# Pools of their own for the hi and the lo tiles of the weights, with lo moved 32 bytes off a multiple of 64

## The chip, the cores and the metric

The kernel runs on one core of a Trainium2 chip. The metric is device microseconds of one execution. Besides the timed runs there is one profiled execution, from which all rows below come: TensorE (PE, with its weight loads as PEld), VectorE (DVE), ScalarE (ACT), GpSimd (POOL), and the DMA queue issued by SyncE (SP).

## The reference

A decoder trunk of two layers on one sequence of 256 tokens, model width 2048, all in float32:

```
for i in range(DEPTH):                       # DEPTH = 2
    h = rmsnorm(x, norm_mix_pre[i])
    m = ssd_mixer(h, ...) if i == 0 else diff_attention(h, ...)
    x = x + rmsnorm(m, norm_mix_post[i])
    h = rmsnorm(x, norm_ffn_pre[i])
    x = x + rmsnorm(swiglu(h, w_gate, w_up, w_down), norm_ffn_post[i])
```

Layer 0 mixes with a Mamba-2 state space block (inner width 4096, 64 heads, chunks of 128), layer 1 with differential attention (16 heads). Each is followed by a SwiGLU network of width 5632. Nearly all arithmetic is in the products of 256 rows with large weight matrices: the input and output projections of the state space block, q/k/v and the output of attention, gate, up and down twice.

## The kernel before

**Products in three parts.** A float32 operand is split into hi, its value rounded to the matmul type float32r, and lo, the rest. A product is hi·hi + hi·lo + lo·hi, three matmuls into the same PSUM accumulator. Activations are split once (`xT_hi`, `xT_lo`, and `ah`/`al` pieces), weights as they come in.

**Weights.** `load` (line 101) brings a block of 128 x 4 x 512 floats (1 MB) into a tile `raw`, of which there are three. `prep` (line 106) makes one hi and one lo tile of 128 x 2 x 512 from half of it: ScalarE writes hi (L113, or L117 where a scale is folded in), VectorE writes lo = raw - hi (L114, L118). Both tiles come from one pool, with four buffers each. In the first part of the kernel there is one such pool, `hlA`; once the state space scan is over and its scratch is given back, a second one, `hlB`, is opened in that place, and tiles are taken from the two in turn.

**Two forms of product.** `mv` (line 143) has the activations as the stationary operand (128 x 128) and the weights as the moving one, 512 columns: L153 runs the three matmuls (x hi, w hi), (x hi, w lo), (x lo, w hi) for each of two 128-row slices. `ws` (line 168) has it the other way round: a 128 x 128 piece of the weights is stationary, and x hi or x lo is moving, 256 columns (L183), in the order (w hi, x hi), (w hi, x lo), (w lo, x hi).

**Order.** The program is written out in full. The order of the work is that of the Python code: `tick` runs small deferred pieces (scan, softmax, transposes, norms) between the steps of the big products. Each engine works through its own list in order and waits for the tiles it needs; buffers come free when their last reader is done.

**Where the tiles lie.** Within a partition, the pools are laid one behind the other. The program of before gives these byte addresses:

| tile | starts at | modulo 64 |
|---|---|---|
| `mhalf`, `table` (4 bytes each) | 18528, 18560 | 32, 0 |
| `xT_hi`, `xT_lo` (4 x 4096 each) | 18944, 35328 | 0 |
| `ones` (512) | 51712 | 0 |
| `dg` (512) | 55264 | 32 |
| `ah`, `al` pieces (8 x 2048 each) | 73216, 89600 | 0 |
| `raw` (3 x 8192) | 105984 | 0 |
| first set: hi, lo (4 x 4096 each) | 130560, 146944 | 0, 0 |
| scan: `mt`/`xg` (5 x 4096), then 8 x 2048 | 163328, 183808 | 0, 0 |
| scan: `dtr` (1024); `u` (2 of 1036) | 203232; 216064, 217120 | 32; 0, 32 |
| later in the scan's place: x rows (8 x 2048), post weights (2 x 2048) | 163328, 179712 | 0, 0 |
| second set: hi, lo (4 x 4096 each) | 183808, 200192 | 0, 0 |
| work tiles of 512 floats (6 x 2048) | 216576 | 0 |

Two gap tiles (`gap1`, line 43, 56 floats; `gap0`, line 88, 88 floats) are there for their size alone.

Of the kernel before, what the change touches and what calls it, by code (L numbers as in the profile page):

```python
# [10 lines left out]
F32 = mybir.dt.float32  # L11
F32R = mybir.dt.float32r
# [4 lines left out]
P = 128  # L17
# [3 lines left out]
KD = D // P  # L21
DI = 4096
NH = 64
# [10 lines left out]
def trunk_kernel(ctx, tc, x_rows, x_cols, vec_cols, vec64, post_rows, lam_rows,  # L34
                 w_zxbc, w_dt, w_so, w_qkv, w_ao,
                 w_g0, w_u0, w_d0, w_g1, w_u1, w_d1, out):
    nc = tc.nc
# [7 lines left out]
    mpool = ctx.enter_context(tc.tile_pool(name="mpool", bufs=8))  # L45
    actp = ctx.enter_context(tc.tile_pool(name="actp", bufs=8))
    rawp = ctx.enter_context(tc.tile_pool(name="rawp", bufs=3))
    hlA = ctx.enter_context(tc.tile_pool(name="hlA", bufs=4))
    accp = ctx.enter_context(tc.tile_pool(name="accp", bufs=4, space=PSUM))
    auxp = ctx.enter_context(tc.tile_pool(name="auxp", bufs=4, space=PSUM))  # L50
    dramp = ctx.enter_context(tc.tile_pool(name="dramp", bufs=1, space=bass.MemoryType.DRAM))
# [42 lines left out]
        sl = slice(t * P, (t + 1) * P)  # L94
        return xT_hi[kt // 4][:, kt % 4, sl], xT_lo[kt // 4][:, kt % 4, sl]

    pools = {"hl": [hlA]}
    seq = [0]
    pending = deque()

# [5 lines left out]
    def prep(raw, scale=None):  # L106
        i = seq[0]
        seq[0] += 1
        pl = pools["hl"][i % len(pools["hl"])]
        hi = pl.tile([P, 2, 512], F32R, tag="hi", name=f"hi{i}")  # L110
        lo = pl.tile([P, 2, 512], F32R, tag="lo", name=f"lo{i}")
        if scale is None:
            nc.scalar.copy(hi, raw)  # L113
            nc.vector.tensor_tensor(lo, raw, hi.bitcast(F32), op=ALU.subtract)  # L114
        else:
            for j in range(2):
                nc.scalar.activation(hi[:, j], raw[:, j], AF.Copy, scale=scale[j])  # L117
                nc.vector.scalar_tensor_tensor(lo[:, j], raw[:, j], scale[j], hi[:, j].bitcast(F32),  # L118
                                               op0=ALU.mult, op1=ALU.subtract)
        return hi, lo  # L120
# [22 lines left out]
    def mv(blocks, stat, evac, lag, scale=None, loaded=()):  # L143
        acc = {}
        last = 2 * len(blocks) - 1

        def run(i, t, hi, lo):
            if i == 0:
                acc[t] = accp.tile([P, 512], F32, tag="acc", name="acc")
            for j in range(2):  # L150
                xh, xl = stat(i, j, t)
                for q, (a, b) in enumerate(((xh, hi), (xh, lo), (xl, hi))):
                    nc.tensor.matmul(acc[t], a, b[:, j], start=(i == 0 and j == 0 and q == 0),  # L153
                                     stop=(i == last and j == 1 and q == 2))
            if i == last:
                evac(t, acc[t])

        for i in range(last + 1):
            if i % 2 == 0:
                raw = loaded[i // 2] if i // 2 < len(loaded) else load(blocks[i // 2])  # L160
            e = 2 * (i % 2)
            hi, lo = prep(raw[:, e:e + 2], scale(i) if scale else None)
            run(i, 0, hi, lo)
            pending.append(lambda i=i, hi=hi, lo=lo: run(i, 1, hi, lo))
            flush(lag)
            tick()

    def ws(blocks, evac):
        flush()
        acc = [accp.tile([P, 512], F32, tag="acc", name="acc") for _ in range(4)]  # L170
        last = 2 * len(blocks) - 1
        for i in range(last + 1):
            if i % 2 == 0:
                raw = load(blocks[i // 2])
            e = 2 * (i % 2)
            hi, lo = prep(raw[:, e:e + 2])
            for ct in range(4):
                cs = slice(ct * P, (ct + 1) * P)
                for j in range(2):
                    kt = i * 2 + j  # L180
                    xh, xl = xT_hi[kt // 4][:, kt % 4], xT_lo[kt // 4][:, kt % 4]
                    for q, (w, xx) in enumerate(((hi, xh), (hi, xl), (lo, xh))):
                        nc.tensor.matmul(acc[ct][:, :S], w[:, j, cs], xx,  # L183
                                         start=(i == 0 and j == 0 and q == 0),
                                         stop=(i == last and j == 1 and q == 2))
                if i == last:
                    evac(ct, acc[ct][:, :S])
            tick()
# [45 lines left out]

    seq[0] += 1
    draw = rawp.tile([P, KD, NH], F32, tag="raw", name="dtraw")
    dhi = hlA.tile([P, KD, NH], F32R, tag="hi", name="dthi")
    dlo = hlA.tile([P, KD, NH], F32R, tag="lo", name="dtlo")
    pdt = accp.tile([P, 512], F32, tag="acc", name="pdt")
    sqs = s2.tile([P, 2, S], F32, tag="t2", name="sqs")  # L240
    for k in range(2):
# [278 lines left out]
    def out_proj(w, first, last, acts, kgs, step, final, lag, t512, pw, scale=None, ns=range(4)):  # L520

        def sums(t, n):
            mt = m[(t, n)]
            row_sumsq(ss4[t][:, n:n + 1], mt, t512("junk"))
            dst = t512("mw") if n == 3 else mt
            (nc.vector if n == 3 else nc.gpsimd).tensor_tensor(dst, mt, pw(n), op=ALU.mult)  # L526
            return dst

        ss4 = {}
        for n in ns:  # L530
            def evac(t, ps, n=n):
                if first:
                    m[(t, n)] = mpool.tile([P, 512], F32, tag="m", name="m")
                    nc.scalar.copy(m[(t, n)], ps)
                else:
                    nc.vector.tensor_tensor(m[(t, n)], m[(t, n)], ps, op=ALU.add)
                if not last:
                    return
                if t not in ss4:
                    ss4[t] = small.tile([P, 4], F32, tag="ss4", name="ss_m", bufs=3)  # L540
                    for e in range(n):
                        sums(t, e)
                dst = sums(t, n)
                if n == 2:
                    p3 = small.tile([P, 1], F32, tag="ss1", name="p3", bufs=3)
                    nc.vector.tensor_reduce(p3, ss4[t][:, 0:3], axis=AX.X, op=ALU.add)
                    nc.vector.tensor_scalar(ss4[t][:, 0:1], p3, 1.0 / D, EPS, op0=ALU.mult, op1=ALU.add)
                if n == 3:
                    norm_chain(t, ss4[t], dst, step, final, t512)

            def stat(i, j, t):
                hi, lo = lookup(acts, (t, kgs[i] // 2))
                jj = (kgs[i] % 2) * 2 + j
                return hi[:, jj], lo[:, jj]

            mv([w[n, kg // 2] for kg in kgs[::2]], stat, evac, lag,
               (lambda i: [scale[:, 2 * kgs[i] + j:2 * kgs[i] + j + 1] for j in range(2)]) if scale is not None else None)
# [27 lines left out]


    postp = ctx.enter_context(tc.tile_pool(name="postp", bufs=1))
    hlB = ctx.enter_context(tc.tile_pool(name="hlB", bufs=4))
    t5 = ctx.enter_context(tc.tile_pool(name="t5", bufs=6))

    def t512(name, shape=(P, 512)):
# [2 lines left out]
    def load_post(ix):  # L594
        def get(n):
            if n not in w:
                w[n] = postp.tile([P, 512], F32, tag="post", name="wpost", bufs=2)
                nc.sync.dma_start(w[n], post_rows[ix, n * 512:(n + 1) * 512].partition_broadcast(P))
            return w[n]

        w = {}
        return get
# [3 lines left out]
            xres[(t, n)] = postp.tile([P, 512], F32, name=f"x_{t}_{n}")  # L606
            nc.sync.dma_start(xres[(t, n)], x_rows[t, :, n * 512:(n + 1) * 512])

    pools["hl"] = [hlA, hlB]
    out_proj(w_so, False, True, ssd_act, list(range(8, 16)), 0, False, LAG, t512, load_post(0), ssd_norm, ns=range(1, 4))  # L610

    def u_stat(i, j, t):
# [199 lines left out]
```

## Time and profile before

| | |
|---|---|
| median of 2 runs | 2618.14 us (2617.39 to 2618.90) |
| the profiled execution | 2617.48 us, its span 2615.7 us |
| granted TensorE clock | 0.997 |
| busy: PE, DVE, ACT, POOL | 99%, 60%, 47%, 6% |
| DMA | 483.35 MB, 185 GB/s on average |

In a row of a group, the name `acc<-lo,xTh` says that the instruction writes tile `acc` and reads `lo` and `xTh`; then come the shapes, the count, the total busy time in us, the mean time of one in ns, and the time for which the engine sat idle just ahead of them, with what ended it. A row of one tile or line gives minimum, median and maximum in ns, and the first and last start in us. A row of waits reads: who waited, for whom, us in total, how many times, the longest. [...]

### The profile page before, as it was taken

To read this page: it belongs to the slowest core of one execution; us is meant where nothing else is said; L and a number is where in the kernel's file an instruction comes from. 1 tells how busy PE (TensorE), PEld (TensorE's weight loads), DVE (VectorE), ACT (ScalarE), POOL (GpSimd) and SP (SyncE) were. 2 spreads that over 40 slices of the span, in tenths; PEclk is the share of its full clock that TensorE was granted. 3 is DMA by queue.
4 is the path that set the end of the run, shared out by engine and by line. 5 is a ranking of instruction groups with operands and counts; after the bars stand their busy time and mean duration, and the time that the engine had idled before them with its cause. 6 is when DMAs were issued, how large, how long until landed. Compare 5 with 4: busy or idle time off the path is not lost.

```text
span 2615.7 us, 34002 instructions
## 1 busy us (share of the span) xinstructions
PE 2589.5 (99%) x13670; PEld 2195.3 (84%) x13670; DVE 1557.1 (60%) x2100; ACT 1241.0 (47%) x1686; POOL 155.6 (6%) x164
## 2 busy tenths in 40 slices
PE   8999999999999999999999999999999999999998
PEld 7988889888888888888888889997788888888886
DVE  8888648887664544455445765556654444555455
ACT  4555555555554444443444644444644444443443
POOL 2031000120100000000001100000100000000002
PEclk9999999999999999999999999999999999999999
DMA  6545555446645555555555543543555555555553
GB/s 223 194 150 199 180 197 179 176 170 218 214 180 193 191 187 193 186 193 193 193 186 192 201 148 143 194 161 136 172 207 193 188 193 187 188 193 193 189 187 131
DMA packets 86653, 483.35 MB, mean 185 GB/s; under 512 B 8096, under 2 KB 24800, under 8 KB 30176
## 3 DMA queue, kind: packets, MB, share of 16 engines
q1 hardware_dynamic: 85840, 480.35, 51.9%
q8 instruction: 107, 1.75, 0.3%
q10 hardware_dynamic: 656, 0.85, 0.1%
q14 instruction: 50, 0.41, 0.0%
HBM read 479.00 MB, written 2.16 MB: 184 GB/s over the span
## 4 chain that ended last, share of the span: by engine, by line
PE 95%; DVE 2%; ACT 1%; issue 1%; POOL 0%; DMA 0%; DVEq 0%; ACTq 0%; POOLq 0%
PE acc L153 73%; PE acc L183 17%; PE pt_f L198 1%; PE sc L688 1%; DVE lo L114 1%; DVE v L349 1%; PE py L424 1%; ACT hi L113 0%; DMA dtraw<-in_w_dt_dram 0%; ACT junk L209 0%; PE pyt L434 0%; ACT xTh L505 0%; PE px L411 0%; PE pst L451 0%; PE po L723 0%
## 5 line engine op out<-in xcount | busy, mean ns | idle before, releaser
L114 DVE TENSOR_TENSOR lo<-raw,hi 128x1024 fp32r<-128x1024 f32 x816 | 1022.1, 1255 | 876.9 <-ACT hi L113 876.1
L113 ACT CAST hi<-raw 128x1024 fp32r<-128x1024 f32 x816 | 856.8, 1052 | 1042.5 <-PE acc L153 813.2
L153 PE MATMUL acc<-hi,xTh 128*128 128x512 f32 x1792 | 710.9, 397 | 1.4 <-ACT xTh L505 1.4
L153 PE MATMUL acc<-hi,xTl 128*128 128x512 f32 x1792 | 704.0, 393 | 0.0
L153 PE MATMUL acc<-lo,xTh 128*128 128x512 f32 x1792 | 701.4, 392 | 2.3 <-DVE lo L114 2.3
L153 PEld LDWEIGHTS acc<-hi,xTh 128*128 128x128 f32 x1792 | 337.1, 188 | 76.2 <-ACT xTh L505 5.3
L153 PEld LDWEIGHTS acc<-lo,xTh 128*128 128x128 f32 x1792 | 337.5, 188 | 73.0 <-DVE lo L114 3.1
L153 PEld LDWEIGHTS acc<-hi,xTl 128*128 128x128 f32 x1792 | 337.0, 188 | 71.5 <-issue 1.3
L183 PE MATMUL acc<-xTh,hi 128*128 128x256 f32 x1280 | 365.9, 286 | 3.4 <-DVE u L345 3.4
L183 PE MATMUL acc<-xTl,hi 128*128 128x256 f32 x1280 | 362.6, 283 | 0.0
L183 PE MATMUL acc<-xTh,lo 128*128 128x256 f32 x1280 | 362.3, 284 | 0.0
L153 PE MATMUL acc<-hi,al_f 128*128 128x512 f32 x704 | 275.4, 391 | 0.0
L153 PE MATMUL acc<-lo,ah_f 128*128 128x512 f32 x704 | 274.3, 390 | 0.0
L153 PE MATMUL acc<-hi,ah_f 128*128 128x512 f32 x704 | 274.2, 390 | 0.0
L183 PEld LDWEIGHTS acc<-xTh,hi 128*128 128x128 f32 x1280 | 245.9, 192 | 4.6 <-DVE u L345 3.8
L183 PEld LDWEIGHTS acc<-xTl,hi 128*128 128x128 f32 x1280 | 245.9, 192 | 0.7 <-issue 0.5
L183 PEld LDWEIGHTS acc<-xTh,lo 128*128 128x128 f32 x1280 | 245.4, 192 | 0.1
L153 PEld LDWEIGHTS acc<-lo,ah_f 128*128 128x128 f32 x704 | 132.2, 188 | 27.5
L153 PEld LDWEIGHTS acc<-hi,al_f 128*128 128x128 f32 x704 | 132.3, 188 | 27.1
L153 PEld LDWEIGHTS acc<-hi,ah_f 128*128 128x128 f32 x704 | 132.3, 188 | 26.9
L118 DVE SCALAR_TENSOR_TENSOR lo<-raw,cols,hi 128x512 fp32r<-128x512 f32 x128 | 92.9, 764 | 61.7 <-ACT hi L117 61.5
L526 POOL TENSOR_TENSOR m<-m,wpost 128x512 f32<-128x512 f32 x24 | 37.1, 1544 | 1510.9 <-ACT junk L209 1503.3
(192 smaller groups left out, 2048.0 us busy)
## 6 DMA issues: line engine op xcount, KB each, us to landing
raw<-in_w_g_dram SPq DMA_DIRECT2D x88, 1024.0 KB, 4.7
raw<-in_w_u_dram SPq DMA_DIRECT2D x88, 1024.0 KB, 4.7
raw<-in_w_d_dram SPq DMA_DIRECT2D x88, 1024.0 KB, 4.8
raw<-in_w_zxbc_dram SPq DMA_DIRECT2D x80, 1024.0 KB, 4.8
raw<-in_w_qkv_dram SPq DMA_DIRECT2D x48, 1024.0 KB, 4.8
raw<-in_w_so_dram SPq DMA_DIRECT2D x32, 1024.0 KB, 4.8
raw<-in_w_ao_dram SPq DMA_DIRECT2D x16, 1024.0 KB, 4.8
mt<-acum_d SPq DMA_DIRECT2D x16, 512.0 KB, 6.6
```

Of the source, the lines that this page charges most:

```text
L113: nc.scalar.copy(hi, raw)
L114: nc.vector.tensor_tensor(lo, raw, hi.bitcast(F32), op=ALU.subtract)
L118: nc.vector.scalar_tensor_tensor(lo[:, j], raw[:, j], scale[j], hi[:, j].bitcast(F32), op0=ALU.mult, op1=ALU.subtract)
L153: nc.tensor.matmul(acc[t], a, b[:, j], start=(i == 0 and j == 0 and q == 0), stop=(i == last and j == 1 and q == 2))
L183: nc.tensor.matmul(acc[ct][:, :S], w[:, j, cs], xx, start=(i == 0 and j == 0 and q == 0), stop=(i == last and j == 1 and q == 2))
L198: nc.tensor.transpose(pt[:, j], src[:, j * P:(j + 1) * P], ident)
L349: nc.vector.scalar_tensor_tensor(v, u[:, k:k + S], cwh[:, ch, k:k + 1], v, op0=ALU.mult, op1=ALU.add)
L424: nc.tensor.matmul(py[e * 64:(e + 1) * 64, a], xd[c][:, 2 * a + e], mts[c][:, 2 * a + e], start=True, stop=True)
L526: (nc.vector if n == 3 else nc.gpsimd).tensor_tensor(dst, mt, pw(n), op=ALU.mult)
L688: nc.tensor.matmul(sc[c][:, h], qT[cp, h, ts], kT[cp, h, :nk * P], start=True, stop=True)
```

## The change

Each set of weight tiles now has one pool for hi and one for lo. Between them, and ahead of the second set, stands a pool with one tile of four floats. The first lo set so starts at 146976, 32 past a multiple of 64. All that lies behind it moves by 32 bytes too: the scan's tiles, then the x rows and post weights. In the second set two more such tiles bring hi to 183872, on a multiple of 64, and lo to 200288, 32 past one; the work tiles then start at 216672, 32 past one. Numbers of buffers, the order of the instructions and the tiles ahead of the first lo set (x, activations, raw, hi) stay as they were. The names of hi and lo tiles get an a or a b for the set.

```diff
-    hlA = ctx.enter_context(tc.tile_pool(name="hlA", bufs=4))
+    hiA = ctx.enter_context(tc.tile_pool(name="hiA", bufs=4))
+    offA = ctx.enter_context(tc.tile_pool(name="offA", bufs=1))
+    gapA = offA.tile([P, 4], F32, name="gapA")
+    nc.gpsimd.memset(gapA, 0.0)
+    loA = ctx.enter_context(tc.tile_pool(name="loA", bufs=4))
...
-    pools = {"hl": [hlA]}
+    pools = {"hl": [(hiA, loA)]}
...
-        hi = pl.tile([P, 2, 512], F32R, tag="hi", name=f"hi{i}")
-        lo = pl.tile([P, 2, 512], F32R, tag="lo", name=f"lo{i}")
+        ab = "ab"[i % len(pools["hl"])]
+        hi = pl[0].tile([P, 2, 512], F32R, tag="hi", name=f"hi{ab}{i}")
+        lo = pl[1].tile([P, 2, 512], F32R, tag="lo", name=f"lo{ab}{i}")
...
-    dhi = hlA.tile([P, KD, NH], F32R, tag="hi", name="dthi")
-    dlo = hlA.tile([P, KD, NH], F32R, tag="lo", name="dtlo")
+    dhi = hiA.tile([P, KD, NH], F32R, tag="hi", name="dthi")
+    dlo = loA.tile([P, KD, NH], F32R, tag="lo", name="dtlo")
...
-    hlB = ctx.enter_context(tc.tile_pool(name="hlB", bufs=4))
+    offB = ctx.enter_context(tc.tile_pool(name="offB", bufs=1))
+    gapB = offB.tile([P, 4], F32, name="gapB")
+    nc.gpsimd.memset(gapB, 0.0)
+    hiB = ctx.enter_context(tc.tile_pool(name="hiB", bufs=4))
+    offC = ctx.enter_context(tc.tile_pool(name="offC", bufs=1))
+    gapC = offC.tile([P, 4], F32, name="gapC")
+    nc.gpsimd.memset(gapC, 0.0)
+    loB = ctx.enter_context(tc.tile_pool(name="loB", bufs=4))
...
-    pools["hl"] = [hlA, hlB]
+    pools["hl"] = [(hiA, loA), (hiB, loB)]
```

## The prediction

> **What bounds the kernel now.** I read the page first, for who fills the span and which chain ended last.
>
> ```profile
> span 2615.7 us, 34002 instructions
> ...
> PE 2589.5 (99%) x13670; PEld 2195.3 (84%) x13670; DVE 1557.1 (60%) x2100; ACT 1241.0 (47%) x1686; POOL 155.6 (6%) x164
> ...
> PE 95%; DVE 2%; ACT 1%; issue 1%; POOL 0%; DMA 0%; DVEq 0%; ACTq 0%; POOLq 0%
> ```
>
> TensorE is busy for 99% of the span and is 95% of the chain that ended last. Busy alone proves little for pipelined matmuls, so I went on to TensorE's own waits; its three longest entries are:
>
> ```profile
> PE acc L183 <- DVE u L345: 3.4, 2, 1.7
> PE acc L153 <- DVE lo L114: 2.3, 2, 2.1
> PE acc L153 <- ACT xTh L505: 1.4, 4, 0.7
> ```
>
> TensorE waits for a lo tile 2.3 us in the whole run. Nothing that merely prepares tiles sooner can gain more than a few us. What can move the time is the pace of the matmuls, so the third view is the timeline of TensorE in two quiet places, the feed-forward (L153, 512 columns) and the q/k projection (L183, 256 columns). First column: start in us.
>
> ```profile
> 1099.61 0.39 PE L153 MATMUL acc<-hi,xTh 128*128 128x512 f32 x1
> 1099.84 0.39 PE L153 MATMUL acc<-lo,xTh 128*128 128x512 f32 x1
> 1100.07 0.39 PE L153 MATMUL acc<-hi,xTl 128*128 128x512 f32 x1
> ...
> 1103.01 0.39 PE L153 MATMUL acc<-hi,xTh 128*128 128x512 f32 x1
> ...
> 1499.72 0.28 PE L183 MATMUL acc<-xTh,hi 128*128 128x256 f32 x1
> ...
> 1501.88 0.28 PE L183 MATMUL acc<-xTh,hi 128*128 128x256 f32 x1
> ```
>
> From 1099.61 to 1103.01 lie 15 steps: 3.40/15 = 0.227 us from start to start. From 1499.72 to 1501.88 lie 18 steps: 2.16/18 = 0.120 us. The step after a lo matmul (1099.84 to 1100.07) is no other than that after a hi matmul. Now the counts, from the groups by form:
>
> ```profile
> L153 PE MATMUL acc<-lo,xTh 128*128 128x512 f32 x1792 | 701.4, 392 | 2.3 <-DVE lo L114 2.3
> ...
> L183 PE MATMUL acc<-xTh,lo 128*128 128x256 f32 x1280 | 362.3, 284 | 0.0
> ...
> L153 PE MATMUL acc<-lo,ah_f 128*128 128x512 f32 x704 | 274.3, 390 | 0.0
> ...
> L153 PE MATMUL acc<-lo,ah_s 128*128 128x512 f32 x256 | 99.8, 390 | 0.0
> ...
> L153 PE MATMUL acc<-lo,ah_o 128*128 128x512 f32 x128 | 49.9, 391 | 0.0
> ```
>
> Lo is the moving operand of 1792+704+256+128 = 2880 matmuls of 512 columns, and the stationary one of 1280 of 256 columns. Each has two hi partners, so 8640 x 0.227 + 3840 x 0.120 = 1961 + 461 = 2422 us, 93% of the span, run at two rigid steps. The kernel is bound by these steps.
>
> **The change, part by part.** The profiled execution took 2617.48 us, 1.8 us over its span; the median shown is 2618.14, 0.7 above it. The sum starts from 2617.5.
>
> The split of the pool as such changes no instruction, no buffer count (four hi and four lo in each set) and no order. It adds three memsets of 128x4 on POOL and moves addresses. The first memset stands at the start, the other two where the second set of buffers is opened.
>
> ```profile
> 0.72 0.14 POOL L44 MEMSET gap<- 128x56 f32 x1 [0.29 <-POOLq L801]
> ...
> 4.60 1.04 POOL L250 TENSOR_TENSOR sqs<-xc 128x512 f32<-128x512 f32 x1 [3.00 <-DMA xc<-in_x_cols_dram]
> ...
> 637.35 0.55 POOL L84 TENSOR_TENSOR rs_g<-ms_g,mhalf 128x1 f32<-128x1 f32 x1 [2.96 <-DVE ms_g L81]
> 656.57 1.30 POOL L526 TENSOR_TENSOR m<-m,wpost 128x512 f32<-128x512 f32 x1 [18.67 <-ACT junk L209]
> ```
>
> A memset of 56 elements took 0.14 us, so one of 4 costs 0.10 to 0.14. Behind the first stand POOL's set-up and its first square, which waits 3.00 us for x anyway: 0 at the end, 0.14 if that wait were gone. The other two fall into the 18.67 us that POOL sits idle between its rows at 637.35 and 656.57: 0. They wait until the scan's buffers under them are free; behind them on POOL stands only that L526, which waits for ACT anyway.
>
> The second hi set now lies 64 bytes higher and its first buffer touches a third scan buffer, the one with the last y. That is read last by the transposes below:
>
> ```profile
> 642.66 0.60 PE L198 MATMUL pt_s<-ident,y 128*128 128x128 f32 x4
> ...
> 653.26 2.56 ACT L117 ACTIVATE hi<-raw,cols 128x512 fp32r<-128x512 f32 x4 [0.42 <-DMA raw<-in_w_so_dram]
> ```
>
> The wait would stand on ACT, ahead of further hi tiles, and TensorE would be the next to feel it. A hi pair takes about 1.3 us there (2.56 for four), so the price is 0 to 1.3 us, once. I take 0, because ACT has the four buffers of the first set to go on with.
>
> What remains is the address of lo itself, and with it those of the tiles laid behind it: scan tiles, x rows, post weights and the 512-wide work tiles, which go from multiples of 64 to 32 past one. What could that cost? First the writer.
>
> ```profile
> L114 DVE TENSOR_TENSOR lo<-raw,hi 128x1024 fp32r<-128x1024 f32 x816 | 1022.1, 1255 | 876.9 <-ACT hi L113 876.1
> ...
> L345 DVE TENSOR_TENSOR u<-acc,rstd_bc x48: 411/419/427, 69.1 to 608.7; 128x256 f32<-128x256 f32 x48
> L347 ACT ACTIVATE v<-u,cbh,cwh x48: 588/602/605, 69.6 to 609.7; 128x256 f32<-128x256 f32 x48
> ```
>
> The conv's two u buffers lie at 216064 (on a multiple of 64) and 217120 (32 past one), and are used in turn. VectorE writes both and ScalarE reads both within 411 to 427 and 588 to 605 ns (minimum and maximum). That bounds the offset at 16/419 = 4% either way: 816 x 1255 x 4% = 41 us of VectorE work, on an engine that idles 877 us ahead of these very instructions, nearly all for hi. At the end it costs nothing; were that cover gone, 41 us.
>
> Then the reader. Two operands of TensorE already lie 32 past a multiple of 64: dg at 55264, the moving operand of L216, and dtr at 203232, a stationary one of L338. Their rows beside rows of the same kind with every operand on a multiple:
>
> ```profile
> L216 PE MATMUL pb<-dg,ones x8: 270/274/377, 38.0 to 1485.6; 128*128 128x128 f32 x8
> ...
> L378 PE MATMUL pcb<-bc x32: 270/275/377, 97.0 to 579.9; 128*128 128x128 f32 x32
> ...
> L338 PEld LDWEIGHTS pdt_tok<-ident,dtr x2: 136/138/139, 61.1 to 61.1; 64*128 64x128 f32 x2
> ...
> L198 PEld LDWEIGHTS pt_f<-ident,a 128*128 128x128 f32 x176 | 19.9, 140 | 10.1 <-DVE a L628 7.4
> ```
>
> Minimum, median and maximum agree within 1 ns for the moving operand, and the weight load is 138 against 140. That is eight and two instructions, in short streams whose recorded ends are modelled, so it does not exclude a price on a stream of 512 columns at full pace. But it is the nearest row: 0 to 1 ns a matmul, 2880 x 1 = 2.9 us at most, of either sign. I take 0. The sum is 2617.5 + 0, on the scale of the median **2618 us**.
>
> [...]
>
> **The rivals.** *Slower: a lo stream pays for straddling.* If operands are fetched in blocks of 64 bytes, a 2048-byte row that starts 32 bytes in touches 33 blocks instead of 32. The mechanism sits in every L153 step with lo: 227/32 = 7.1 ns x 2880 = 20 us. In L183 lo is loaded as weights, 512 bytes, 9 blocks instead of 8.
>
> ```profile
> L183 PEld LDWEIGHTS acc<-xTh,lo 128*128 128x128 f32 x1280 | 245.4, 192 | 0.1
> L153 PEld LDWEIGHTS acc<-lo,xTh 128*128 128x128 f32 x1792 | 337.5, 188 | 73.0 <-DVE lo L114 3.1 <-issue 3.0
> ```
>
> A load is recorded at 192 ns against a step of 120, so loads overlap, and an eighth more, 24 ns, is paid in full or hidden: 0 to 1280 x 24 = 31 us. Together 20 to 51 us: 2638 to 2669, some 2642 if most of the load hides. The other moved tiles add some 800 small matmuls at perhaps 7 ns, 6 us more. For it: all long streams are aligned today, so the trace cannot deny it at full pace. Against it: the dg and dtr rows. It passes 2% from 52/2880 = 18 ns per lo stream on, two and a half times the block price.
>
> *Faster: hi and x on one address phase disturb each other.* Two steps of 256 columns are 240 ns, one of 512 is 227, so 13 ns of each step do not scale with columns. Weights and stream now start on the same phase; if that is where the 13 ns come from, the 2880 + 1280 matmuls with lo shed up to 13 ns each: 54 us, 2564. If half, 2591. For it: weight loads beside a long stream take 188 ns, those of the transposes 140 (rows above), so the two are not quite independent. Against it: the step behind lo equals that behind hi, and the dg row, whose weights are on a multiple and whose stream is not, shows no gain.
>
> [...]
>
> *It does not do what it says.* Were the 16-byte gap laid so that lo still starts on a multiple of 64, nothing is tried: 2618. In the program of before four-byte tiles are laid 32 bytes apart (18528, 18560), so I think little of this.
>
> **How the numbers follow.** No price: 0.62, at 2613 to 2623. Not moved: 0.05, the same time. Slower by straddling: 0.20, of which 0.11 below 2650, 0.02 up to the 2% bound, 0.07 beyond it. Faster by phase: 0.13, of which 0.04 above 2600, 0.06 down to 2%, 0.03 beyond. Within 2% is about what a measurement of this kernel can tell from no change. The range 2600 to 2650 holds 0.62 + 0.05 + 0.11 + 0.04 = 0.82. The likeliest case alone is 2613 to 2623. Faster 0.03, same 0.90, slower 0.07.
>
> **What the profile after would show.** If I am right: the start-to-start step is again 0.227 us behind lo as behind hi, and 0.120 in L183; L114 stays at 1255 ns within 4%; TensorE's waits for hi or lo stay at a few us. The straddling rival shows as steps of 0.234 behind each lo stream and 0.227 behind hi, the faster one as 0.214 to 0.220. Memsets that matter would show as new POOL entries in TensorE's waits. The prediction is wrong if a step moves by more than 2 ns (2 x 4160 = 8 us), or if ACT's hi tiles start to wait for scan buffers again and again.

## The result, and the profile after

The changed kernel takes **2649.31 us**, median of 2 runs (2647.29 to 2651.32), against 2618.14 before: ratio 1.0119, interval 1.0076 to 1.0163. It is 31 us slower. That is within 2%, but far outside what the two kernels' runs scatter, and the prediction of no change was wrong.

The page of the kernel after first. Its groups of VectorE's lo tiles and of TensorE's matmuls now come one for each set; the names that end in a belong to the first set, those in b to the second.

```profile
span 2649.5 us, 34007 instructions
...
PE 2623.9 (99%) x13670; PEld 2193.5 (83%) x13670; DVE 1556.4 (59%) x2100; ACT 1236.9 (47%) x1686; POOL 156.0 (6%) x167
...
PE 94%; DVE 3%; ACT 1%; issue 1%; DMA 0%; POOL 0%; DVEq 0%; SPq 0%; ACTq 0%; POOLq 0%
...
L119 DVE TENSOR_TENSOR loa<-raw,hia 128x1024 fp32r<-128x1024 f32 x488 | 620.2, 1273 | 475.1 <-ACT hia L118 474.9
...
L119 DVE TENSOR_TENSOR lob<-raw,hib 128x1024 fp32r<-128x1024 f32 x328 | 401.8, 1225 | 430.8 <-ACT hib L118 430.8
...
L158 PE MATMUL acc<-loa,xTh 128*128 128x512 f32 x1024 | 408.1, 399 | 0.2 <-DVE loa L119 0.2
...
L158 PE MATMUL acc<-lob,xTh 128*128 128x512 f32 x768 | 304.5, 397 | 0.0
```

TensorE is busy 34.4 us longer (2623.9 against 2589.5) in a span that is 33.8 us longer (2649.5 against 2615.7). The other engines work as long as before: VectorE 1556.4 against 1557.1 us, ScalarE 1236.9 against 1241.0. So the loss lies on TensorE. Its three longest waits:

```profile
PE pdt L272 <- DVE xTl L268: 3.5, 4, 1.4
PE acc L188 <- DVE u L350: 3.4, 2, 1.7
PE pdt L272 <- DVE dtlo L197: 1.6, 1, 1.6
```

No wait has grown into anything near 34 us. What is left is the pace of the matmuls, so here is the timeline of TensorE in the same two quiet places (L153 has become L158, L183 has become L188).

```profile
1112.72 0.40 PE L158 MATMUL acc<-hib,xTh 128*128 128x512 f32 x1
1112.95 0.39 PE L158 MATMUL acc<-lob,xTh 128*128 128x512 f32 x1
1113.18 0.40 PE L158 MATMUL acc<-hib,xTl 128*128 128x512 f32 x1
1113.42 0.39 PE L158 MATMUL acc<-hib,xTh 128*128 128x512 f32 x1
...
1116.19 0.39 PE L158 MATMUL acc<-hia,xTh 128*128 128x512 f32 x1
...
1518.04 0.28 PE L188 MATMUL acc<-xTh,hia 128*128 128x256 f32 x1
...
1520.18 0.28 PE L188 MATMUL acc<-xTh,hib 128*128 128x256 f32 x1
```

The records overlap: a 512-column one lasts 0.39 or 0.40 us, and the next starts 0.23 or 0.24 us after it, so the pace is read from the starts and not from the durations. From 1112.72 to 1116.19 lie 15 steps: 3.47/15 = 0.231 us, where it was 0.227. From 1518.04 to 1520.18 lie 18: 2.14/18 = 0.119, where it was 0.120. The order of the matmuls is the same as before; the 512-column ones simply follow each other more slowly. Single rows, rounded to 0.39 and 0.40 us, hardly show it; the means of the groups do: 399 and 397 ns for the lo streams beside `xTh`, where it was 392.

Over the whole trace, from the start of a matmul to the start of the next of the same form (intervals over 280 ns for 512 columns and over 180 ns for 256 left out, since they hold a wait), the means in ns are:

| | hi to hi | hi to lo | lo to hi | all, 512 columns | all, 256 columns |
|---|---|---|---|---|---|
| before | 227.5 | 227.2 | 227.2 | 227.3 | 119.9 |
| after | 229.8 | 232.1 | 234.7 | 232.2 | 118.4 |

"hi" and "lo" say which weight tile streams. 4.9 ns x 8640 = +42 us, and -1.5 ns x 3840 = -6 us: +36 us together, for a span that grew by 33.8. The two step lengths hold the whole loss. Two things in this table fit no step of the prediction: the steps behind hi are slower too, and the 256-column steps are faster. As for hi, the two sets differ. In the first set hi stayed where it was, and a step from hi to hi takes 228.8 ns (1239 steps). In the second set hi moved by 64 bytes, from 183808 to 183872, and it takes 231.7 ns (843 steps).

### The profile page after: what moved, and what is told of

Its sections match the earlier page's. It is cut to its first block, busy times and chain, and to the rows that moved or that the text cites. A ratio compares the mean times of both kernels' runs of the same rounds, so it can differ in the third digit from the quotient of the medians.

```text
span 2649.5 us, 34007 instructions
## 1 busy us (share of the span) xinstructions
PE 2623.9 (99%) x13670; PEld 2193.5 (83%) x13670; DVE 1556.4 (59%) x2100; ACT 1236.9 (47%) x1686; POOL 156.0 (6%) x167
## 4 chain that ended last, share of the span: by engine, by line
PE 94%; DVE 3%; ACT 1%; issue 1%; DMA 0%; POOL 0%; DVEq 0%; SPq 0%; ACTq 0%; POOLq 0%
PE acc L158 74%; PE acc L188 16%; PE pt_f L203 1%; PE sc L700 1%; DVE loa L119 1%; DVE v L354 1%; PE py L429 1%; PE po L735 0%; ACT junk L214 0%; PE pyt L439 0%; ACT xTh L510 0%; PE pst L456 0%; DMA raw<-in_w_qkv_dram 0%; PE px L416 0%; PE pyo L462 0%
## 5 line engine op out<-in xcount | busy, mean ns | idle before, releaser
L119 DVE TENSOR_TENSOR loa<-raw,hia 128x1024 fp32r<-128x1024 f32 x488 | 620.2, 1273 | 475.1 <-ACT hia L118 474.9
L118 ACT CAST hia<-raw 128x1024 fp32r<-128x1024 f32 x488 | 511.2, 1048 | 587.9 <-PE acc L158 432.0
L119 DVE TENSOR_TENSOR lob<-raw,hib 128x1024 fp32r<-128x1024 f32 x328 | 401.8, 1225 | 430.8 <-ACT hib L118 430.8
L118 ACT CAST hib<-raw 128x1024 fp32r<-128x1024 f32 x328 | 344.0, 1049 | 486.9 <-PE acc L158 413.9
L158 PE MATMUL acc<-hia,xTh 128*128 128x512 f32 x1024 | 413.4, 404 | 0.7 <-ACT xTh L510 0.7
L158 PE MATMUL acc<-loa,xTh 128*128 128x512 f32 x1024 | 408.1, 399 | 0.2 <-DVE loa L119 0.2
L158 PE MATMUL acc<-hia,xTl 128*128 128x512 f32 x1024 | 401.5, 393 | 0.0
L158 PE MATMUL acc<-hib,xTh 128*128 128x512 f32 x768 | 305.5, 398 | 0.7 <-ACT xTh L510 0.7
L158 PE MATMUL acc<-hib,xTl 128*128 128x512 f32 x768 | 305.1, 397 | 0.0
L158 PE MATMUL acc<-lob,xTh 128*128 128x512 f32 x768 | 304.5, 397 | 0.0
L188 PE MATMUL acc<-xTh,hia 128*128 128x256 f32 x1024 | 291.6, 285 | 3.4 <-DVE u L350 3.4
L188 PE MATMUL acc<-xTh,loa 128*128 128x256 f32 x1024 | 289.4, 284 | 0.0
L188 PE MATMUL acc<-xTl,hia 128*128 128x256 f32 x1024 | 287.7, 281 | 0.0
L158 PEld LDWEIGHTS acc<-hia,xTh 128*128 128x128 f32 x1024 | 192.8, 188 | 51.8 <-ACT xTh L510 4.0
L158 PEld LDWEIGHTS acc<-hia,xTl 128*128 128x128 f32 x1024 | 192.6, 188 | 45.9 <-DVE xTl L511 0.7
L158 PEld LDWEIGHTS acc<-loa,xTh 128*128 128x128 f32 x1024 | 193.0, 188 | 42.6 <-issue 3.2
L188 PEld LDWEIGHTS acc<-xTh,hia 128*128 128x128 f32 x1024 | 193.4, 189 | 4.7 <-DVE u L350 3.8
L188 PEld LDWEIGHTS acc<-xTl,hia 128*128 128x128 f32 x1024 | 194.8, 190 | 0.6 <-issue 0.5
L188 PEld LDWEIGHTS acc<-xTh,loa 128*128 128x128 f32 x1024 | 194.0, 190 | 0.1
L158 PEld LDWEIGHTS acc<-hib,xTh 128*128 128x128 f32 x768 | 144.5, 188 | 35.0 <-ACT xTh L510 1.6
L158 PEld LDWEIGHTS acc<-hib,xTl 128*128 128x128 f32 x768 | 144.7, 188 | 33.3 <-issue 0.7
L158 PEld LDWEIGHTS acc<-lob,xTh 128*128 128x128 f32 x768 | 144.3, 188 | 31.7
```

Of the source, the lines that this page charges most:

```text
L188: nc.tensor.matmul(acc[ct][:, :S], w[:, j, cs], xx, start=(i == 0 and j == 0 and q == 0), stop=(i == last and j == 1 and q == 2))
```

## The experiments

The question was which property of the addresses sets the step. Is it where lo itself starts, and on what raster; is it that all else behind it moved; or is it how the streaming tile lies to the stationary one? All edits below are on the changed kernel, and no run leaves work out. "Distance" is the address of the stationary tile less that of the streaming one, modulo 256 bytes (why 256 is seen below). Unless another time is named, a kernel stands against the kernel before on the same chip: 2618.3 us for the first four runs, 2617.27 for the next four, 2616.96 for three, 2617.32 for the last.

**Is it the 32 bytes?** Gaps of 64 bytes instead of 16 keep every tile on a multiple of 64.

```diff
-    gapA = offA.tile([P, 4], F32, name="gapA")
+    gapA1 = offA1.tile([P, 16], F32, name="gapA1")
...
-    gapB = offB.tile([P, 4], F32, name="gapB")
+    gapB0 = offB0.tile([P, 16], F32, name="gapB0")
...
-    gapC = offC.tile([P, 4], F32, name="gapC")
+    gapB2 = offB2.tile([P, 16], F32, name="gapB2")
```

> Pools split as in the change, but every gap is 64 bytes, so that lo, hi and all tiles behind them start on a multiple of 64. Theory A (the address of lo is the cause): back to the time before, 2618 us, steps of 227 ns in L158 and 120 ns in L188. Theory B (the split of the pool itself, by its order or its buffers): 2649 us stays.

Measured: 2644.14 us, ratio 1.0101 [1.0086, 1.0116]. Nothing straddles a 64-byte block any more, and nearly the whole loss is still there. Steps: 231.7 and 117.6 ns. So the raster is not 64.

**Is it the tiles behind lo?** A further gap of four floats behind each lo pool puts all that follows back on a multiple of 64; the gap ahead of the second hi set is then not needed and is left out.

```diff
     loA = ctx.enter_context(tc.tile_pool(name="loA", bufs=4))
+    offA3 = ctx.enter_context(tc.tile_pool(name="offA3", bufs=1))
+    gapA3 = offA3.tile([P, 4], F32, name="gapA3")
+    nc.gpsimd.memset(gapA3, 0.0)
...
     loB = ctx.enter_context(tc.tile_pool(name="loB", bufs=4))
+    offB3 = ctx.enter_context(tc.tile_pool(name="offB3", bufs=1))
+    gapB3 = offB3.tile([P, 4], F32, name="gapB3")
+    nc.gpsimd.memset(gapB3, 0.0)
```

> Only lo starts 32 past a multiple of 64; scan tiles, x rows, post weights and work tiles are put back on multiples of 64 by further gaps. Theory A (the streams of lo pay): 2649 us as in the changed kernel, within 3 us. Theory C (the other moved tiles pay): 2618 us. In between, the shares of the two are read off.

Measured: 2650.43 us, 1.0122 [1.0107, 1.0137]; steps 232.2 and 118.3 ns, as after. Hi and lo lie at the same remainders modulo 256 as in the changed kernel, the scan tiles, x rows, post weights and work tiles do not, and the time is the same: those tiles play no part that can be seen.

**Hi and lo both off, and hi alone off.** The first has its gap ahead of hi and none between, the second one ahead of hi and one ahead of lo, so that hi lies at 32 and lo on a multiple of 64.

```diff
+    gapA0 = offA0.tile([P, 4], F32, name="gapA0")
     hiA = ctx.enter_context(tc.tile_pool(name="hiA", bufs=4))
-    gapA = offA.tile([P, 4], F32, name="gapA")
     loA = ctx.enter_context(tc.tile_pool(name="loA", bufs=4))
+    gapA3 = offA3.tile([P, 4], F32, name="gapA3")
...
```

> Hi and lo both start 32 past a multiple of 64, all other tiles on one. Theory A1 (each moving stream off 64 pays for straddling, by itself): three streams of a triple pay instead of one, so about 2618 + 3 x 31 = 2711 us, and each L158 step is 234 ns or more. Theory A2 (only a change of offset from one moving stream to the next pays): there is no change any more within a triple, 2618 us and steps of 227 ns.

```diff
+    gapA0 = offA0.tile([P, 4], F32, name="gapA0")
     hiA = ctx.enter_context(tc.tile_pool(name="hiA", bufs=4))
-    gapA = offA.tile([P, 4], F32, name="gapA")
+    gapA2 = offA2.tile([P, 4], F32, name="gapA2")
     loA = ctx.enter_context(tc.tile_pool(name="loA", bufs=4))
...
```

> The mirror image: hi starts 32 past a multiple of 64, lo and all else on one. Theory A1 (each stream off 64 pays for itself): two streams of three pay, 2618 + 2 x 31 = 2680 us, the steps of the lo streams stay at 227 ns. Theory A2 (a change of offset between streams pays): as many changes as in the changed kernel, 2649 us.

Measured: 2655.80 us, 1.0144 [1.0129, 1.0159], and 2651.46, 1.0127 [1.011, 1.0144]. A price for each moved stream would have made the first three times as dear as the change (three streams of a product instead of one) and the second twice. They cost 37.5 and 33.2 us against 31. The theory that only a change of offset between successive streams pays is out as well: it gave 2618 us for both off (its 2649 for hi alone came true). The steps: 233.0 with both off; with hi off, 233.7 behind hi (hi to hi) and 230.5 behind lo, much like the mirror of after. In after and with hi off, the dearest step is the one behind the tile at 32 (in the first set of after 235.4 ns, behind lo), but its neighbours pay too (228.8 hi to hi and 231.6 hi to lo in that set, 227.5 and 227.2 before).

**The split alone.** All three gaps are gone, the pools stay split.

```diff
-    gapA = offA.tile([P, 4], F32, name="gapA")
-    nc.gpsimd.memset(gapA, 0.0)
...
-    gapB = offB.tile([P, 4], F32, name="gapB")
-    nc.gpsimd.memset(gapB, 0.0)
...
-    gapC = offC.tile([P, 4], F32, name="gapC")
-    nc.gpsimd.memset(gapC, 0.0)
```

> The pools are split as in the change, but without any gap, so that every tile has the address of before (all on multiples of 512). Theory B (the split itself costs): about 2644 us, as with gaps of 64. Theory D (addresses decide, by a larger block than 64): 2618 us, steps of 227 and 120 ns.

Measured: 2617.27 us, 1.0000 [0.999, 1.0009]; steps 227.3 and 119.9. The split costs nothing. It is the addresses.

**Which addresses?** Without the gaps, the first set's four lo buffers are spread over different remainders modulo 512: 0, 128, 256 and 384 in one kernel, 0, 32, 64 and 96 in the other. The long tile is used only over its first 1024 floats. (`lamv` moves to a work tile to make room.)

```diff
-        lo = pl[1].tile([P, 2, 512], F32R, tag="lo", name=f"lo{ab}{i}")
+        if ab == "a":
+            lo = pl[1].tile([P, 1056], F32R, tag="lo", name=f"lo{ab}{i}")[:, :1024].rearrange("p (j n) -> p j n", j=2)
+        else:
+            lo = pl[1].tile([P, 2, 512], F32R, tag="lo", name=f"lo{ab}{i}")
```

> Pools split; in the first set the four lo buffers start at 0, 128, 256 and 384 past a multiple of 512, hi and the second set on multiples (the small lamv tile moves to a work tile to make room). Theory D with blocks of 512: the steps around the lo buffers at 128, 256 and 384 are 230 to 236 ns, those around the one at 0 are 227; about 2635 us. With blocks of 128: all steps 227 ns, 2618 us. Theory B: 2644 us with no difference between the buffers.

The other kernel is the same with `[P, 1032]`, and with a gap of 96 floats ahead of the second set.

> As before, with the four lo buffers of the first set at 0, 32, 64 and 96 past a multiple of 512. Theory D: the steps around the buffer at 0 are 227 ns, those around the others 230 ns and more, by the block that holds: with blocks of 64 those at 0 and 64 are alike. Theory B: no difference between the buffers, 2644 us.

Measured: 2620.80 and 2633.18 us, one run each. The first is the clear one. The step behind lo, by the address of the buffer from which lo streams:

| lo streams from | 0 | 128 | 256 | 384 |
|---|---|---|---|---|
| step behind it, ns | 227.3 | 233.8 | 227.1 | 233.8 |

(some 400 steps each; at 0 1576, with those of the second set). Zero and 256 are alike, 128 and 384 are alike: 256 bytes further on the step is the same within 0.2 ns, 128 further on it differs by 6.5 to 6.7. Over these four addresses it repeats after 256 bytes; that this is a period at other addresses too is the author's inference, and all distances below are taken by it. In the 32-byte ladder the step behind lo was 234.7 at 32, 233.0 at 64 and 231.4 at 96, but the hi steps behind them spread over 229 to 235, so that it settles less.

Taken modulo 256, the first kernels moved more than their names say, since the gaps add up. The activations are at 0 in all of these:

| kernel | first set: hi, lo | second set: hi, lo |
|---|---|---|
| after | 0, 32 | 64, 96 |
| lo moved by 64 | 0, 64 | 128, 192 |
| lo by 32, rest on 64 | 0, 32 | 64, 96 |
| hi by 32 | 32, 64 | 96, 128 |
| hi and lo by 32 | 32, 32 | 96, 96 |

So "hi by 32" has its lo tiles off a multiple of 256 as well, and in none of the five is the second hi set on one.

**Whose address: that of lo, or that of lo against x?** One kernel moves `xT_hi` and `xT_lo` by 32 bytes, and with them only the small tiles between them and the activation pieces; the other moves them and everything behind them by the same 32 bytes. Both are without the change's gaps.

```diff
-    gap1 = gapp.tile([P, 56], F32, name="gap1")
+    gap1 = gapp.tile([P, 48], F32, name="gap1")
...
-    gap0 = const.tile([P, 88], F32, name="gap0")
+    gap0 = const.tile([P, 96], F32, name="gap0")
```

> Pools split without gaps; only the activations xT_hi and xT_lo start 32 past a multiple of 512, all weights on one. Theory D1 (the place of the streamed operand by itself): L158, where x is stationary, keeps 227 ns; L188, where x is streamed, changes. Theory D2 (stream and weight load disturb each other by their relative place): L158 with x goes to 230 to 236 ns as in the changed kernel, L158 with the other activations (still on multiples) keeps 227 ns; about 2618 + 5376 x 5 ns = 2645 us.

```diff
-    gap0 = const.tile([P, 88], F32, name="gap0")
+    gap0 = const.tile([P, 96], F32, name="gap0")
```

> Pools split without gaps, and everything from xT_hi on (activations, raw, hi, lo, scan and work tiles) moved by 32 bytes together, so that nothing large lies on a multiple of 64 any more, but streamed operand and loaded weights keep their distance of a multiple of 256. Theory D1 (a stream off 64 pays for itself): 2655 us as with hi and lo both off, or more. Theory D2 (only the distance between stream and weight load counts): 2617 us, steps of 227 and 120 ns.

Measured: with x alone moved 2632.87 us, 1.0059 [1.0044, 1.0074]; with all moved together 2616.81, 1.0001 [0.9992, 1.001]. No weight tile moved in the first, and it is slower; everything, lo included, lies 32 past a multiple of 64 in the second, and it costs nothing. So in these two runs the price does not go with the address of lo or of x by itself, but with the distance. The timeline of the kernel with x alone moved shows it inside one execution, since `ah` and `al` were not moved:

```profile
920.07 0.39 PE L155 MATMUL acc<-hib,ah_f 128*128 128x512 f32 x1
...
922.79 0.39 PE L155 MATMUL acc<-hia,ah_f 128*128 128x512 f32 x1
...
1103.23 0.40 PE L155 MATMUL acc<-hia,xTh 128*128 128x512 f32 x1
...
1106.73 0.40 PE L155 MATMUL acc<-hia,xTh 128*128 128x512 f32 x1
...
1509.98 0.28 PE L185 MATMUL acc<-xTh,hib 128*128 128x256 f32 x1
...
1512.07 0.28 PE L185 MATMUL acc<-xTh,hia 128*128 128x256 f32 x1
```

The same weights stream past `ah_f` in 2.72/12 = 0.227 us a step (distance 0) and past `xTh` in 3.50/15 = 0.233 (distance 32). Over the trace these are 227.0 ns (3149 steps) and 233.2 ns (5020 steps). Where the stationary tile changes from an `ah` or `al` piece to x, the step ahead of the change already takes 234.9 ns (51 steps; 227.5 with the split alone), though its own pair is at distance 0: here the step goes with the next matmul's stationary tile too. The 256-column steps, where x streams and the weights are stationary (distance -32 = 224), are at 2.09/18 = 0.116 instead of 0.120. The forecast of 2645 us had the dearer 512-column steps alone; the 3840 steps of 256 columns gained 3.2 ns each, 12 us. And the timeline with everything moved together, in the place where x is stationary:

```profile
1099.84 0.39 PE L155 MATMUL acc<-hib,xTh 128*128 128x512 f32 x1
...
1103.24 0.39 PE L155 MATMUL acc<-hib,xTh 128*128 128x512 f32 x1
```

3.40/15 = 0.227 again.

**The period, put to the test.** With 128-byte gaps every lo tile is at 128 from a multiple of 256, and hi on one.

```diff
-    gapA = offA.tile([P, 4], F32, name="gapA")
+    gapA1 = offA1.tile([P, 32], F32, name="gapA1")
...
-    gapB = offB.tile([P, 4], F32, name="gapB")
+    gapB0 = offB0.tile([P, 32], F32, name="gapB0")
...
-    gapC = offC.tile([P, 4], F32, name="gapC")
+    gapB2 = offB2.tile([P, 32], F32, name="gapB2")
```

> Lo starts 128 past a multiple of 256 in both sets, hi and the activations on one. Theory D2 with a period of 256 and the step sizes of the ladder: each of the 2880 steps behind a lo stream takes 234 instead of 227 ns, the others stay: +20 us, and the L188 steps lose about 1 ns, -3 us: 2634 us. If a period of 128 held: 2617 us. If the spreading to the hi steps seen with 32 and 64 appears here too: 2645 us.

Measured: 2657.73 us, 1.0152 [1.0137, 1.0168], the slowest of all and above each of the three forecasts. The timeline of this kernel:

```profile
1117.69 0.40 PE L158 MATMUL acc<-hib,xTh 128*128 128x512 f32 x1
...
1121.19 0.40 PE L158 MATMUL acc<-hia,xTh 128*128 128x512 f32 x1
```

3.50/15 = 0.233 over hi and lo together. That 128 is off, as the ladder said, holds; that only the step behind lo pays, as there, does not: here the means are 230.3 hi to hi, 234.5 hi to lo and 233.3 lo to hi. With every lo off, the neighbours pay too; with two of the first set's four buffers off, they did not.

**Each form at the distance it likes.** So far the 512-column step was shortest at distance 0 (227.0 ns, against 233.2 at 32), the 256-column step off it (116.7 ns at 224, against 119.9 at 0). In the first set, each tile is now longer than its data, and the view into it is chosen by the form that will use it, so that one buffer serves both. (`lamv` again moves to a work tile.) The first kernel puts it at 128 in the 256-column form and at 0 in the other.

```diff
+    def view(pool, which, far, name):
+        k = turn_a[0] % 4
+        o = 32 if (k % 2 == 1) != far else 0
+        t = pool.tile([P, 1056], F32R, tag=f"{which}{k}", name=name, bufs=1)
+        return t[:, o:o + 1024].rearrange("p (j n) -> p j n", j=2)
...
-            hi, lo = prep(raw[:, e:e + 2])
+            hi, lo = prep(raw[:, e:e + 2], far=True)
```

> All on multiples of 256 in L158's form, where weights are streamed; where they are loaded as the stationary operand (L188's form) the tiles of the first set are used 128 bytes further on, by a view into tiles 128 bytes longer. Theory D2: L158 keeps 227 ns, and the 3072 L188 steps of the first set go from 120 to 114 ns (the step measured at a distance of 128 for both hi and lo): 2617 - 18 = 2599 us. If the distance helps L188 only by 1 to 3 ns: 2608 to 2614 us. Theory D1: no change, 2617 us.

Measured: 2612.76 us, 0.9985 [0.9976, 0.9994]. Faster than the kernel before, but by 4 us where 18 were hoped for: the 256-column step at distance 128 is 118.8 ns here, and not 114.0. That figure was the mean of only 251 steps of the kernel with 64-byte gaps, from hi to hi in the second set, where hi was at 128 and lo at 192 (and not both at 128, as the expectation has it); with the steps to and from lo that set's mean was 116.3. The distance of a matmul's own pair does not settle this step alone. The second kernel takes the distance with the surer number, 224, the one with x alone moved. To make room it also drops `gap1`, shortens `gap0` and lets the two `rh0` columns share a tile.

```diff
+    def view(pool, which, far, name):
+        k = turn_a[0] % 4
+        o = k * 8
+        if which == "lo":
+            o = o + 24 if far else o + 32
+        elif far:
+            o = (k + 7) % 8 * 8
+        t = pool.tile([P, 1080], F32R, tag=f"{which}{k}", name=name, bufs=1)
+        return t[:, o:o + 1024].rearrange("p (j n) -> p j n", j=2)
...
```

> As the version with views 128 bytes further on, but where the weights of the first set are stationary they lie at a distance of 224 (256 less 32) from the streamed activations, the distance that all L188 steps had when the activations were moved by 32; in L158's form all stays at a distance of 0 modulo 256. Theory D2: 3072 L188 steps take 116.7 instead of 119.9 ns, -9.8 us: 2607 us. If the gain was tied to the activations' own place: 2613 to 2617 us.

Measured: **2607.46 us, 0.9962 [0.9948, 0.9975]**, as expected. The timeline of this kernel (L169 is the 512-column form, L199 the other):

```profile
370.28 0.39 PE L169 MATMUL acc<-hia,ah_s 128*128 128x512 f32 x1
...
372.32 0.39 PE L169 MATMUL acc<-hia,ah_s 128*128 128x512 f32 x1
...
378.96 0.28 PE L199 MATMUL acc<-xTh,hia 128*128 128x256 f32 x1
...
381.06 0.28 PE L199 MATMUL acc<-xTh,hia 128*128 128x256 f32 x1
```

2.04/9 = 0.227 for 512 columns, untouched, and 2.10/18 = 0.117 for 256. Over the trace the latter is 117.0 ns at distance 224 (2949 steps) and 119.7 at 0 (those of the second set). 2.7 ns x 2949 = 8 us of the 9.9 gained. This version beats the kernel before by 10 us and the changed one by 42.

All the steps together, in ns, beside the time:

| kernel | hi to hi | hi to lo | lo to hi | 512, all | 256, all | us |
|---|---|---|---|---|---|---|
| split alone | 227.3 | 227.1 | 227.4 | 227.3 | 119.9 | 2617.27 |
| all moved by 32 | 227.4 | 227.1 | 227.3 | 227.3 | 119.9 | 2616.81 |
| lo ladder of 128 | 227.2 | 227.5 | 229.1 | 228.0 | 119.6 | 2620.80 |
| lo ladder of 32 | 229.9 | 229.8 | 230.6 | 230.1 | 119.0 | 2633.18 |
| x alone moved by 32 | 231.0 | 230.8 | 230.8 | 230.9 | 116.7 | 2632.87 |
| lo moved by 64 | 232.2 | 231.8 | 231.1 | 231.7 | 117.6 | 2644.14 |
| lo by 32, rest on 64 | 229.7 | 232.3 | 234.5 | 232.2 | 118.3 | 2650.43 |
| hi by 32 | 233.7 | 232.6 | 230.5 | 232.3 | 118.6 | 2651.46 |
| hi and lo by 32 | 232.6 | 233.0 | 233.4 | 233.0 | 118.4 | 2655.80 |
| lo moved by 128 | 230.3 | 234.5 | 233.3 | 232.7 | 119.1 | 2657.73 |
| views, 256-column form at 128 | 227.2 | 227.2 | 227.3 | 227.3 | 119.1 | 2612.76 |
| views, 256-column form at 224 | 227.4 | 227.1 | 227.4 | 227.3 | 117.5 | 2607.46 |

## Why the prediction was wrong, step by step

**The bound was right.** Two rigid steps carry 93% of the span, and the whole loss is in these two steps, not in a wait. The tell-tale that the prediction set itself, a step that moves by more than 2 ns, is what went off: the 512-column step moved by 4.9. That the time still lies within the stated 2600 to 2650, by 0.7 us, is luck: it is there by way of the straddling rival, whose mechanism failed (below). The prediction also held that a measurement can hardly tell 2% from no change; the intervals here are 0.1 to 0.5% to either side.

**POOL at nothing: right.** The three memsets, in the groups of the kernel after:

```profile
L51 POOL MEMSET gapA<- 128x4 f32 x1 | 0.1, 101 | 0.0
...
L599 POOL MEMSET gapC<- 128x4 f32 x1 | 0.1, 101 | 5.9 <-DVE yo L464 5.9
L595 POOL MEMSET gapB<- 128x4 f32 x1 | 0.1, 101 | 5.6 <-PE pt_s L203 5.6
```

101 ns each, at the low end of 0.10 to 0.14 us. They wait 5.6 and 5.9 us for the scan's last readers, in POOL's idle time. TensorE has no wait for POOL or for hi among its longest, so the wait of 0 to 1.3 us for the second hi set was rightly taken at 0 (its new address was another matter, see below); and the split without gaps costs 0.0 us.

**The writer at nothing: right.** lo takes 1273 ns in the first set and 1225 in the second, (488 x 1273 + 328 x 1225)/816 = 1254 on average, against 1255. The bound of 4% was wide, and no price shows.

**The reader at 0 to 1 ns a matmul: this step failed.** It was read from the dg row, 270/274/377 against 270/275/377, and carried over to 2880 matmuls of 512 columns. The price was 4.9 ns, on 8640 of them, and -1.5 ns on 3840. The row could not carry this. It holds eight matmuls of 128 columns, in runs of two, with float32 operands, and not a full stream of loads and 512-column matmuls in float32r. And its spread of 270 to 377 ns is wide beside the price: 4.9 ns in 512 columns would be about 1 ns in 128, an estimate that supposes that the price goes with the columns. It was not for want of the right pair: dg at 55264 streams past ones at 51712, distance 32 modulo 256, which took the long stream with x moved to 233.2 ns. The prediction did say that this row "does not exclude a price on a stream of 512 columns at full pace"; it still gave the case 0.62. The bound of this step should have been the one worked out from the stream itself, which the rivals held. A second term went with it: the move of the second hi set by 64 bytes was priced as a wait alone, and its new address, again a multiple of 64, was given no price; with every tile on a multiple of 64 (2644.14) the loss was 26 us.

**The rival "slower by straddling" had the sign and the size, not the mechanism.** It forecast 2638 to 2669, and 2649 lies inside, by luck. For a stream that touches one more 64-byte block cannot explain a loss of 26 us with every tile on 64 (2644.14), nor no loss at all with every tile 32 past it (2616.81). Its own sign, 0.234 behind lo and 0.227 behind hi, came half true: 234.7 behind lo, but 229.8 and 232.1 behind hi, and in the first set, where hi had not moved, 228.8 and 231.6.

**The rival "faster by phase" had the right pair and, for the main term, the wrong sign.** In these runs the step went with how weights and stream lie to each other, as it said. For 256 columns the distances off 0 were faster, 119.9 to 118.4 here and to 116.7 with x alone moved. For 512 columns they were slower, 227.0 to 233.2 with x alone moved. The 13 ns that do not scale with columns are not shed. That weights and stream are not quite independent, which it read from 188 against 140 ns, showed in the steps: in one execution, weights at the same addresses stream at 227.0 ns a step past stationary tiles at distance 0 and at 233.2 past those at distance 32. The prediction's argument against this rival, that the step behind lo equals that behind hi, had no force: before the change all long streams had distance 0, so the trace held no other case of them.

**What stays open.** Why steps from hi to hi, with hi at distance 0, pay as well when every lo is off (228.8 ns in the first set of after, 230.3 with lo at 128), and did not in the ladder of 128 (227.2). Why one distance has more than one price: behind a first-set lo tile 64 bytes past a multiple of 256 the step was 229.3 ns in "hi by 32", 231.4 in "lo moved by 64" and 233.0 in the ladder of 32. Why 256 columns at distance 128 took 114.0 ns from hi to hi in one kernel and 118.8 in another. So in these runs the time changed only where distances changed, and with 0 throughout the 512-column step stayed at 227.3 ns; they give no formula for the price. What inside the chip makes it was not measured.

## What to carry to other kernels

Where TensorE runs a full stream of float32r matmuls with a new weight load for each, look at how the stationary and the streaming tile lie to each other modulo 256 bytes in a partition, not at whether each is aligned: here all tiles moved together cost nothing (2616.81 us), and the activations or the weights moved against each other cost 16 to 41 us of 2617. A pool inserted ahead of others moves them, so an edit that leaves every matmul as it is can change the pace: here the mean step of 512 columns went from 227.3 to 232.2 ns. When a trace is asked for such a price, read the steps from start to start in a long stream of the same form; a short run of small matmuls (a median of 274 ns for `dg` at distance 32, beside 275 in the row it was read against), or a single recorded duration (0.39 or 0.40 us), hardly showed it here.

## What the runs showed of the hardware that was not expected

- The step of a 512-column matmul went with the distance of its two operands' addresses: 227.0 ns at 0, 233.2 at 32 (3149 and 5020 steps of one execution).
- In the ladder of 128 the step repeated after 256 bytes: 227.3, 233.8, 227.1, 233.8 ns behind lo at 0, 128, 256, 384.
- The 256-column form went the other way: 119.7 ns at 0, 117.0 at 224, in one execution.
- The price spread to steps whose own pair was at 0: with a third of the 512-column streams off (lo at 128, hi at 0 in both sets) the mean step is 232.7 ns (230.3 hi to hi), with all of them off (hi and lo by 32) 233.0.
